# A written order for the queues of four engines, in place of the scheduler's, in a bidirectional hybrid encoder on one core

## The chip, the cores and the metric

One NeuronCore of a Trainium2 chip runs the whole program, in one launch. A core has five engines that run side by side, each taking its own queue of instructions strictly in order: TensorE (PE in the profile: matmuls, with the loads of its weights as PEld), VectorE (DVE), ScalarE (ACT), GpSimd (POOL) and SyncE (SP), whose queue here only issues transfers (DMA) from the chip's memory. Engines wait for one another by semaphores.

The metric is the device time of one execution in microseconds (us), smaller is better.

## What is computed

The reference is an encoder with two layers over a sequence of 512 tokens of width 1024, all in float32. Each layer is a token mixer and an MLP, and each adds its result to the scaled input and normalizes:

```python
for i in range(DEPTH):                       # DEPTH = 2
    if i % N_MIXERS == 0:
        m = _mixer_gdn(x, ...)               # layer 0: gated DeltaNet, 8 heads of 128
    else:
        m = _mixer_gla(x, ...)               # layer 1: gated linear attention, 4 heads, keys 128, values 256
    x = _layernorm(DEEPNORM_ALPHA * x + m, ln1_g[i], ln1_b[i])
    x = _layernorm(DEEPNORM_ALPHA * x + _sq_relu_mlp(x, mlp_w1[i], mlp_w2[i]), ln2_g[i], ln2_b[i])

def _sq_relu_mlp(h, w1, w2):                 # w1: 1024 x 4096, w2: 4096 x 1024
    a = jax.nn.relu(jnp.matmul(h, w1))
    return jnp.matmul(a * a, w2)
```

Both mixers project x, run a recurrence over the tokens in both directions (in chunks of 64 in the reference), add the two, normalize each head (RMS), multiply with a SiLU gate, and project back.

## The kernel before, in words

**Precision.** Every large matmul is done as three (`mm3`, lines 130 to 136): both operands are split into a rounded high part and a remainder, and high·high (L133), high·low (L135, or its mirror) and low·high (L136) are summed in PSUM. So each weight block comes into a buffer `wst` by a transfer that SP issues (`dma`, L46), is cast by ScalarE to `wh` (L104) and has its remainder `wl` made by VectorE (L105). `split` has a second form for blocks with a home of their own (`wb`, L98 and L99). These two steps, some hundreds of times, are the largest groups of both engines.

**Stages.** In the order of the trace: loading and transposing x with the first small projections (to 38 us); the gated DeltaNet of layer 0 with its output projection (to 430); the MLP of layer 0 (to 735); gated linear attention, GLA (to 1005); the MLP of layer 1 (to 1329); the last normalization and its stores (to 1337.6). The MLPs, and the values of GLA, use seven products of half-size blocks in place of eight, for which sums of weight blocks are made by VectorE (L485 and others) or by transfers that GpSimd issues and that add into their target (`ch`, `wst`: L1058, L1068; `w2r`: L600).

**The places that the prediction speaks of.** In the head, `ws` (L148) is a stack of high and low parts of the small weights for the projection `bap` (L154), and `xtl` (L208) the low part of the transposed x. In GDN, SP loads the blocks of the output projection, and `z`, the input again, for the residual (`load_z`, called in `output` of `gdn`); the place of z is freed by an instruction of the head that used it (`p`, L1951). In GLA, `GlaHead.levels` scales q and k for a tree of block sizes (qh L1223, kh L1226, with the running products E L1242 and F L1245), multiplies them (`scp`, L1212) and copies the result into `sc` under a mask (L1250 to L1256). `GlaHead.states` makes the states (stp L1292, copied to `st` by ScalarE at L1295, later ones by VectorE at L1298) and the outputs (op L1308); ScalarE copies each to `o` (L1310) and squares it back into its bank of PSUM (L1311), and only then can PE write to that bank, which it shares with `scp`. `GlaHead.norm` scales `o` on VectorE (L1322) by `rs` and the gate in `vs`, and PE transposes it (`otp`, L1326). `rs` comes out of a chain of small steps on VectorE and ScalarE (`rsqrt`, L243 to L260). `GlaValues.products` runs the seven products (`pjv`) with weights out of `ch`. At the end of each MLP, `layernorm` (L286 to L289) makes `xt`, which PE transposes (`tp`, L195).

**What sets the order.** The program is traced in the order in which its Python runs, with hand-made interleaving: a planner with due times in `gdn`, the tables FILL and STEPS in `gla`, generators in `mlp`. A scheduler then decides each engine's order from priorities and readiness by its own estimates. At some places the kernel takes that freedom away: `in_order(engine)` chains all instructions of one engine that were traced in its body. It stands around stretches of PE at six places, once around GpSimd's constants, once around GpSimd's work in the MLP, and once around a stretch of ScalarE there. `after` adds single waits that pace transfers. The chain that `in_order` adds is one of order alone: it has no semaphore and costs no instruction.

Of the kernel before, what the change touches and what calls it, by code (L numbers as in the profile page):

```python
# [28 lines left out]
class Ctx:  # L29
# [23 lines left out]
    def after(self, ins, before):  # L53

        self.tc.add_manual_dep(
            ins.ins, before.ins.name, mybir.DependencyInfo(mybir.DependencyClass.Sync, mybir.DependencyReason.DATA),
            reason="paced")
        return ins

    @contextlib.contextmanager  # L60
    def in_order(self, engine):
# [267 lines left out]
    def out_last(self, w, ks, lhs, z, tags, par, homes=None, xtags=("tp",), late=0, room=None):  # L329

        nc = self.nc
        homes = iter(homes or [None] * len(ks))
        ws = [[self.wrows(w, k * P, hf * 512, next(homes)) for k in ks[::2]] for hf in range(2)]
        banks = {}
        self.cols = room and (par, room)

        def part(t, hf, js):
            sl = slice(t * P, (t + 1) * P)
            if (t, hf) not in banks:
                banks[t, hf] = self.bank([P, 512], F32, name="ob", tag=tags[(2 * t + hf) % len(tags)])  # L340
                if not room:
                    nc.tensor.matmul(banks[t, hf], self.ident, z[t][hf], start=True, stop=False)
            for i in js:
                ah, al = lhs(ks[i], sl)
                wh, wl = ws[hf][i // 2]
                self.mm3(banks[t, hf], ah, al, wh[:, i % 2, :], wl[:, i % 2, :], room is not None and i == 0, i == len(ks) - 1)

        n, m = len(ks), len(ks) // 2
        with self.in_order(mybir.EngineType.PE) if late else contextlib.nullcontext():
            if late:  # L350
                for t in range(2):
                    for hf in range(2):
                        part(t, hf, range(m))
            for t in range(NT):
                for hf in range(2):
                    part(t, hf, range(m if late and t < 2 else 0, n))
                    if hf == 0 and 0 < late <= t:
                        self.xpose(t - late, self.xt[t - late], xtags)
                    if room:
                        nc.vector.tensor_tensor(self.xh(t)[hf], z[t][hf], banks[t, hf], ALU.add)  # L360
                if room:
                    self.whiten(self.xh(t))
                else:
                    self.layernorm([banks[t, hf] for hf in range(2)], self.xh(t), par, last=late and t == NT - 1)
                if not late:
                    self.xpose(t, self.xt[t], xtags)
        return [t for t in range(NT - late, NT)]


def mlp(c, w1, w2, g, b, left, before=None, out=None):  # L370
# [13 lines left out]
    with c.banks(pj=2, X=2, Y=2, Z=2), tc.tile_pool(name="mlp", bufs=2) as pool:  # L384
# [372 lines left out]
        for j, t in enumerate(left):  # L757
            for q, run in enumerate(c.xposes(t, "Y", "Z")):
                between[(2, 4 * q) if j == len(left) - 1 else (0, 4 + 3 * q)] = run
        with c.in_order(mybir.EngineType.PE), c.in_order(mybir.EngineType.Pool):  # L760
            hs = {0: h}
            tail = last(G - 1, hs)
            units = seconds(hs, tail)
            halves = c.proj_halves(specs, between)
            for f, ps in enumerate(halves):
                done = act(ps, h[0][:, f, :])
                load_part(0, 0, f // 2, f % 2, done if f > 1 else None)
                if f == 0 and before:
                    lnp.extend(c.load_ln(*before, ln_tile(), acts[0]))
                    c.cols = None  # L770
            combo = combos()
            def run(n):
                for _ in range(n):
                    next(combo, None)
            op = next(combo)
            work = pairs(op, hs)
            run(3)
            w = c.wcols(w1, GF // 2 * P)
            for f in range(4, GF):
                nw = c.wcols(w1, (f + 1) * P) if f + 1 < GF else None  # L780
                run(1 if f == 6 else 2)
                done = feature(f, h, w)
                w = nw
                if f in (4, 5):
                    load_part(0, 1, 1, f % 2, done)
                if f == 5:
                    load(0, 1, 0, acts[-1])
                if f == 6:
                    next(units)
                    next(work)  # L790
            not_done.clear()
            for _ in combo:
                pass
            with c.in_order(mybir.EngineType.Activation):
                for _ in work:
                    next(units)
                next(units, None)
            par.extend(c.load_ln(g, b, ln_tile(), acts[-1]))
            for _ in tail:
                pass  # L800


def load_x(c, x, tags, zero):
    c.new_xt()
    c.new_x()
    for t in range(NT):
        c.dma(c.xt[t], x[t * P:(t + 1) * P, :])
    idle = c.bank([P, S], F32, name="idle", tag="pj")

    def warm(n=1):  # L810
        for _ in range(n):
            c.nc.tensor.matmul(idle, zero[:, 0, :], zero[:, 0:NT, :], start=True, stop=True)

    with c.in_order(mybir.EngineType.PE):
        warm(7)
        c.marks = [c.xpose(t, c.xt[t], tags, warm=warm if t < NT - 1 else None) for t in range(NT)]
    return c.marks[-1]
# [52 lines left out]
def gla(c, gc, w_in, gate_w2, w_out, cols):  # L870
# [5 lines left out]
    with c.banks(ac=2, tp=2, X=2, Y=2), tc.tile_pool(name="gla", bufs=2) as pool, \  # L876
# [11 lines left out]
        c.dma(gst, w_in[:, base:base + 32].rearrange("(k p) n -> p k n", p=P))  # L888
        specs = [(c.stack(gst, 3), "gps", "ac")]
        specs += [(c.wcols(w_in, c0), nm, "XY"[nm == "pjk"]) for c0, nm in ((0, "pjq"), (H * P, "pjk"))]  # L890
        with c.in_order(mybir.EngineType.PE):
            gps, *qk0 = c.proj_halves(specs, dict(zip(((2, 0), (2, 4)), c.xposes(NT - 1, "tp", "tp"))))
        low = slice(64, 96)
        gl3 = pool.tile([P, S], F32R, name="gl3", tag="gl3", bufs=1)
# [19 lines left out]
        lhs = lambda k, sl: tuple(t[:, k % 4, sl] for t in o_pair(k // 4))  # L914
        early = list(range(KT // 2))
        vr = GlaValues(c, pool, w_in, heads)
        with c.in_order(mybir.EngineType.PE):
            list(heads[0].qk(qk0))
            heads[0].gates(0)
            heads[0].gates(1)  # L920
# [59 lines left out]
class GlaValues:  # L980


    ORDER = (1,2,5,6,7,4,3)
# [352 lines left out]
class GdnConst:  # L1336


    def __init__(self, c, pool, pz, w_in, a_log, dt_bias, conv_w, norm_g, behind):
# [11 lines left out]
        V.memset(self.eps[:, 1:2], math.log(0.5 * P * RMS_EPS))  # L1351
        self.ng = pool.tile([P, 1], F32, name="ng", bufs=1)
        self.cw = pool.tile([P, 5, 24], F32, name="cw", bufs=1)
        with c.in_order(mybir.EngineType.Pool):
            self.gates(w_in, a_log, dt_bias, conv_w, norm_g, behind)
            self.masks()

# [63 lines left out]
    def gates(self, w_in, a_log, dt_bias, conv_w, norm_g, behind):  # L1421

        c, pool = self.c, self.pool
# [27 lines left out]
            nc.tensor.transpose(ps[:, :120], cw, c.ident[:120, :120])  # L1451
            V.tensor_copy(self.cw, ps[:, :120].rearrange("p (k t) -> p k t", k=5))

        with c.in_order(mybir.EngineType.PE):
            ps, self.k0 = c.proj_halves([(ws, "bap", "ch"), (k0, "pjk", "ac")], {(1, 6): taps})
        yr = pool.tile([2 * M, S], F32, name="yr", tag="E", bufs=2)
        nc.scalar.copy(yr, ps[:2 * M, :])
# [501 lines left out]
        "b_gate_b", "b_norm_g", "b_w_out", "ln1_g", "ln1_b", "mlp_w1", "mlp_w2", "ln2_g", "ln2_b"]  # L1959


def body(tc, nc, a, out):
    with contextlib.ExitStack() as es:
        def pool(name, bufs, **kw):
# [2 lines left out]
        c = Ctx(tc, nc, (pool("const", 1), pool("big", 1), pool("wst", 4), pool("whl", 3), pool("small", 3)))  # L1967
        x = a["x"][0]
        with tc.tile_pool(name="gcst", bufs=1) as gp:
# [5 lines left out]
            left = gla(c, gc, a["b_w_in"][0], a["b_gate_w2"][0], a["b_w_out"][0], cols)  # L1975
        mlp(c, a["mlp_w1"][1], a["mlp_w2"][1], a["ln2_g"][1], a["ln2_b"][1], left,
            (a["ln1_g"][1], a["ln1_b"][1]), out=out[0])


# [16 lines left out]
```

## Time and profile before

| | |
|---|---|
| three runs | 1342.2, 1340.04, 1339.14 us; median 1340.04 |
| the profiled execution | 1339.26 us |
| its span in the trace | 1337.6 us (1.66 us lie around it) |
| granted TensorE clock | 0.998 |
| moved by DMA | 148.86 MB, mean 111 GB/s |

The profile is one execution, recorded instruction by instruction. A row of the timeline gives the start in us, the duration in us, the engine, the line and operation, the tile written and the tiles read (buffer numbers left out), their shapes, and the number of equal instructions that the row stands for; in brackets the idle time of the engine ahead of it and the instruction that ended it. An engine can show over 90% busy and still be fed late: the view of waits lists, for one engine, whom it stood idle for, and how long. A window row gives, for a stretch, each engine's busy us and count, the granted clock, the DMA engines' share and GB/s.

### The profile page before, as it was taken

Reading aid. Unit: us, or ns where it says so; the run is one execution under the profiler, and the core shown is the slowest. Engines: PE = TensorE matmul, PEld = TensorE weight load, DVE = VectorE, ACT = ScalarE, POOL = GpSimd, SP = SyncE. Lnnn points to the kernel's source line nnn. Section 1 sums busy time; section 2 is a strip of 40 time slices with the busy share of each in tenths; the row PEclk is TensorE's granted clock in tenths of the full one; section 3 lists DMA queues with packets and bytes.
Section 4 is the critical chain, followed back from the end, with each engine's and each line's share of the span. In section 5 each row is a group of like instructions: output and inputs, shape, how many; then the busy total and the mean of one; then the engine's idle time right before and its main releaser. Section 6 shows DMA issues by size and latency. Waiting matters only on the chain.

```text
span 1337.6 us, 22200 instructions
## 1 busy us (share of the span) xinstructions
PE 1312.5 (98%) x8726; PEld 1127.9 (84%) x8726; DVE 1127.6 (84%) x1738; ACT 777.7 (58%) x1477; POOL 118.8 (9%) x180
## 2 busy tenths in 40 slices
PE   8999999999999999999999999999999999999997
PEld 7778887888888899999998878877879899999986
DVE  6798898998768897988977889888877998889875
ACT  4766667666534656656563358647357556566640
POOL 6600000000001000101001011110000001001000
PEclk9999999999999999999999999999999999999999
DMA  7321111211133765556521666464125665556411
GB/s 196 79 64 49 49 49 48 64 46 47 52 111 110 196 135 152 130 160 160 124 83 63 183 140 158 101 152 126 44 68 156 176 173 145 139 156 129 126 63 48
DMA packets 155289, 148.86 MB, mean 111 GB/s; under 512 B 7425, under 2 KB 124193, under 8 KB 155184
## 3 DMA queue, kind: packets, MB, share of 16 engines
q1 hardware_dynamic: 144416, 115.62, 29.2%
q0 software_dynamic: 10624, 31.55, 12.6%
q8 instruction: 68, 1.11, 0.3%
q14 instruction: 37, 0.30, 0.1%
q10 hardware_dynamic: 144, 0.26, 0.1%
HBM read 118.06 MB, written 4.19 MB: 91 GB/s over the span
## 4 chain that ended last, share of the span: by engine, by line
PE 82%; DVE 7%; ACT 5%; DMA 3%; issue 2%; SPq 0%; POOL 0%; DVEq 0%; ACTq 0%; POOLq 0%
PE pq L136 6%; PE pq L133 6%; PE pq L135 6%; PE pX L135 3%; PE pX L136 3%; PE pX L133 3%; PE pjv L133 2%; PE pjv L135 2%; PE pjv L136 2%; PE pl L136 2%; PE pl L133 2%; PE pl L135 2%; PE op L1926 2%; PE lv L1789 2%; PE pY L135 2%; PE pY L136 2%
## 5 line engine op out<-in xcount | busy, mean ns | idle before, releaser
L104 ACT CAST wh<-wst 128x1024 fp32r<-128x1024 f32 (+1 forms) x175 | 173.2, 994 | 134.9 <-DVE wst L485 47.5
L105 DVE TENSOR_TENSOR wl<-wst,wh 128x1024 fp32r<-128x1024 f32 (+1 forms) x175 | 201.4, 1153 | 24.7 <-ACT wh L104 23.7
L105 DVE TENSOR_TENSOR w2l<-w2r,w2h 128x1024 fp32r<-128x1024 f32 x84 | 102.6, 1221 | 25.5 <-ACT w2h L104 25.2
L136 PE MATMUL pq<-xth,wl 128*128 128x256 f32 x384 | 108.5, 283 | 0.0
L133 PE MATMUL pq<-xth,wh 128*128 128x256 f32 x384 | 108.5, 283 | 0.0
L135 PE MATMUL pq<-xtl,wh 128*128 128x256 f32 x384 | 108.5, 283 | 0.0
L104 ACT CAST w2h<-w2r 128x1024 fp32r<-128x1024 f32 x84 | 88.1, 1049 | 5.1 <-PE pZ L136 2.6
L136 PE MATMUL pq<-t,wl 128*128 128x256 f32 x288 | 81.2, 282 | 0.4 <-DVE wl L105 0.4
L133 PE MATMUL pq<-t,wh 128*128 128x256 f32 x288 | 81.0, 281 | 0.3 <-DVE h L532 0.3
L135 PE MATMUL pq<-t,wh 128*128 128x256 f32 x288 | 81.1, 281 | 0.0
L135 PEld LDWEIGHTS pq<-xtl,wh 128*128 128x128 f32 x384 | 73.4, 191 | 3.0
L133 PEld LDWEIGHTS pq<-xth,wh 128*128 128x128 f32 x384 | 73.3, 191 | 2.9
L135 PE MATMUL pX<-w2l,ah 128*128 128x512 f32 x192 | 75.5, 393 | 0.0
L136 PE MATMUL pX<-w2h,al 128*128 128x512 f32 x192 | 75.4, 393 | 0.0
L133 PE MATMUL pX<-w2h,ah 128*128 128x512 f32 x192 | 75.1, 391 | 0.0
L136 PEld LDWEIGHTS pq<-xth,wl 128*128 128x128 f32 x384 | 73.3, 191 | 0.0
L600 POOL DMA_DIRECT2D w2r<-w2r x36 | 31.0, 877 | 404.3 <-DVE w2l L105 191.3
L485 DVE TENSOR_TENSOR wst<-wst 128x512 f32<-128x512 f32 x96 | 64.9, 684 | 0.2
L105 DVE TENSOR_TENSOR al<-h,ah 128x1024 fp32r<-128x1024 f32 x42 | 51.2, 1220 | 9.2 <-ACT ah L104 9.2
L133 PEld LDWEIGHTS pq<-t,wh 128*128 128x128 f32 x288 | 54.4, 189 | 1.6 <-DVE h L532 0.7
L135 PEld LDWEIGHTS pq<-t,wh 128*128 128x128 f32 x288 | 54.3, 188 | 1.0
L136 PEld LDWEIGHTS pq<-t,wl 128*128 128x128 f32 x288 | 54.3, 188 | 0.6 <-DVE wl L105 0.6
(557 smaller groups left out, 4049.9 us busy)
## 6 DMA issues: line engine op xcount, KB each, us to landing
wst<-in_mlp_w SPq DMA_DIRECT2D x64, 512.0 KB, 4.8
w2r<-in_mlp_w SPq DMA_DIRECT2D x64, 512.0 KB, 3.8
w2r<-w2r POOLq DMA_DIRECT2D x36, 512.0 KB, 5.6
wst<-in_a_w_in SPq DMA_DIRECT2D x32, 512.0 KB, 4.1
wst<-in_b_w_in SPq DMA_DIRECT2D x24, 256.0 KB, 3.3
wst<-in_a_w_out SPq DMA_DIRECT2D x8, 512.0 KB, 3.7
wst<-in_b_w_in SPq DMA_DIRECT2D x8, 512.0 KB, 5.5
ch<-wst POOLq DMA_DIRECT2D x8, 512.0 KB, 5.8
```

Of the source, the lines that this page charges most:

```text
L104: nc.scalar.copy(hi, src)
L105: self.low = nc.vector.tensor_tensor(lo, src, hi.bitcast(F32), ALU.subtract)
L133: mm(ps, ah, bh, start=start, stop=False, **kw)
L135: mm(ps, ah, bl, start=False, stop=False, **kw)
L136: mm(ps, al, bh, start=False, stop=stop, **kw)
L485: V.tensor_tensor(a, a, b, ALU.add)
L600: nc.gpsimd.dma_start(a, b, accum_op=ALU.add)
L1789: T.matmul(ps[:, u, :, :], lhs[:, u, :], cols(rhs, u, s, i), start=True, stop=True)
L1926: T.matmul(op[:, n, :], l, r, start=i == 0, stop=i == len(mm) - 1)
```

## The change

All uses of `in_order` are replaced by an empty context, and the freedom is taken away altogether: at the end of `body`, a new method chains all instructions of each engine in an order that is written down as a table of indices into the traced instructions of that engine. Nothing is computed in another way; the same instructions stand in both programs. The tables were found by a search that used the durations of a trace. The order of PE in the table is the one that it had.

```diff
+    def written_order(self, orders):
+
+        traced = list(self.nc.cur_bb.bb.instructions)
+        for name, text in orders.items():
+            own = [i for i in traced if i.engine == getattr(mybir.EngineType, name)]
+            ends = [[int(k) for k in run.split("-")] for run in text.split()]
+            seq = [own[k] for run in ends for k in range(run[0], run[-1] + 1)]
+            for prev, i in zip(seq, seq[1:]):
+                self.tc.add_manual_dep(
+                    i, prev.name, mybir.DependencyInfo(mybir.DependencyClass.NoSync, mybir.DependencyReason.DATA),
+                    reason="in_order")
...
-        with self.in_order(mybir.EngineType.PE) if late else contextlib.nullcontext():
+        with contextlib.nullcontext():
...
-        with c.in_order(mybir.EngineType.PE), c.in_order(mybir.EngineType.Pool):
+        with contextlib.nullcontext():
...
-            with c.in_order(mybir.EngineType.Activation):
+            with contextlib.nullcontext():
...
+ORDER = {
+    "PE": """
+        0-129 134-196 130-133 197-209 226-237 246-248 210-213 257-259 268-270 287-292 309-314 323-325 342-347 356-358
...
+    "Pool": """
+        0 2-13 15-17 19-50 52 54 56-57 63 67-68 64-66 70-72 69 73-80 58 81-96 59-62 97-131 133 132 134 137 140 135-136
...
         mlp(c, a["mlp_w1"][1], a["mlp_w2"][1], a["ln2_g"][1], a["ln2_b"][1], left,
             (a["ln1_g"][1], a["ln1_b"][1]), out=out[0])
+        c.written_order(ORDER)
```

The table has five parts: PE, DVE, Activation (ScalarE), Pool (GpSimd) and SP. From line 59 of the kernel on, the lines of the changed kernel are 12 higher (L104 becomes L116, L1322 becomes L1334).

What the tables do to the queues is read from the two programs. Three places follow; a row is a line, an operation, the tile written and the tiles read, and a shape.

ScalarE near the end of GLA, in the last head, before (in the trace at 928 to 937 us). `o` and `op` are an output of the recurrence and its bank of PSUM, `F<-wst` is the cast of a weight block of the output projection into a place where F stood:

```order
L98 CAST wb<-wst 128x1024
L104 CAST wh<-wst 128x1024
L1187 COPY k<-pjk 128x512
L1219 ACTIVATE ge<-k 128x512
L1310 COPY o<-op 128x256
L1311 ACTIVATE op,ss<-o 128x256
L104 CAST F<-wst 128x1024
L1310 COPY o<-op 128x256
L1311 ACTIVATE op,ss<-o 128x256
L1250 COPY sc<-scp 128x512
```

And in the changed kernel, the same place and, after the dots, the one where that cast now stands:

```order
L1322 COPY o<-op 128x256
L1199 COPY k<-pjk 128x512
L1231 ACTIVATE ge<-k 128x512
L110 CAST wb<-wst 128x1024
L1322 COPY o<-op 128x256
L1323 ACTIVATE op,ss<-o 128x256
L1262 COPY sc<-scp 128x512
...
L1340 ACTIVATE oth<-otp,gcol 128x512
L110 CAST wb<-wst 128x1024
L116 CAST F<-wst 128x1024
```

The cast into F, which stood between two pairs of copy and square, now comes behind the outputs' copies, the steps of `rsqrt` and the first `oth`.

VectorE in the same head, before (946 to 950 us). `rst` and `rs` are steps of `rsqrt`, the four `o` are scaled by `rs`, `xt` takes in a piece of the output projection, `qh` and `kh` are operands of the next level:

```order
L1253 COPY_PREDICATED sc<-mu_1043,scp 128x512
L259 TENSOR_TENSOR rst<-rst,rsv 128x4
L1223 TENSOR_TENSOR qh<-q,F 128x512
L325 SCALAR_TENSOR_TENSOR xt_10647<-xt_10647,oa 128x512
L260 SCALAR_TENSOR_TENSOR rs<-rst,rsy 128x4
L1226 TENSOR_TENSOR kh<-k,E 128x512
L1322 SCALAR_TENSOR_TENSOR o<-o,rs,vs 128x256 x4
L1242 TENSOR_TENSOR E<-E,F 128x2x16x16
```

And in the changed kernel:

```order
L271 TENSOR_TENSOR rst<-rst,rsv 128x4
L1265 COPY_PREDICATED sc<-mu_1036,scp 128x512
L272 SCALAR_TENSOR_TENSOR rs<-rst,rsy 128x4
L1257 TENSOR_TENSOR F<-F 128x32x2x8
L1238 TENSOR_TENSOR kh<-k,E 128x512
L1334 SCALAR_TENSOR_TENSOR o<-o,rs,vs 128x256 x4
L1235 TENSOR_TENSOR qh<-q,F 128x512
L1254 TENSOR_TENSOR E<-E,F 128x2x16x16
```

The `qh` of the next level and the piece into `xt` stood ahead of `rs` and of the four `o`; now `qh` is behind them, and `xt` is further back.

SP's queue in GDN, before, and then in the changed kernel: `wst` are the blocks of GDN's output projection (`in_a_w_out`) and of the MLP's first matrix, `z` is the input for the residual:

```order
L46 DMA wst<-in_a_w_in 128x8x128 x32
L46 DMA wst<-in_a_w_out 128x2x512 x7
L46 DMA z<-in_x 128x512 x4
L46 DMA wst<-in_a_w_out 128x2x512
L46 DMA wst<-in_mlp_w 128x8x128 x2
L46 DMA z<-in_x 128x512 x4
```

```order
L46 DMA wst<-in_a_w_in 128x8x128 x32
L46 DMA wst<-in_a_w_out 128x2x512 x3
L46 DMA z<-in_x 128x512
L46 DMA wst<-in_a_w_out 128x2x512
L46 DMA z<-in_x 128x512
L46 DMA wst<-in_a_w_out 128x2x512
L46 DMA z<-in_x 128x512 x2
L46 DMA wst<-in_a_w_out 128x2x512 x3
L46 DMA z<-in_x 128x512 x4
L46 DMA wst<-in_mlp_w 128x8x128 x6
```

The first four loads of z stood behind seven loads of weights, and the first of them now stands behind three.

More of the change, by code (lines that the diff above doesn't have):

```diff
@@ L812, in warm @@
             c.nc.tensor.matmul(idle, zero[:, 0, :], zero[:, 0:NT, :], start=True, stop=True)
-    with c.in_order(mybir.EngineType.PE):
+    with contextlib.nullcontext():
         warm(7)
@@ L890, in gla @@
         specs += [(c.wcols(w_in, c0), nm, "XY"[nm == "pjk"]) for c0, nm in ((0, "pjq"), (H * P, "pjk"))]
-        with c.in_order(mybir.EngineType.PE):
+        with contextlib.nullcontext():
             gps, *qk0 = c.proj_halves(specs, dict(zip(((2, 0), (2, 4)), c.xposes(NT - 1, "tp", "tp"))))
@@ L916, in gla @@
         vr = GlaValues(c, pool, w_in, heads)
-        with c.in_order(mybir.EngineType.PE):
+        with contextlib.nullcontext():
             list(heads[0].qk(qk0))
@@ L1353, in __init__ @@
         self.cw = pool.tile([P, 5, 24], F32, name="cw", bufs=1)
-        with c.in_order(mybir.EngineType.Pool):
+        with contextlib.nullcontext():
             self.gates(w_in, a_log, dt_bias, conv_w, norm_g, behind)
@@ L1452, in taps @@
             V.tensor_copy(self.cw, ps[:, :120].rearrange("p (k t) -> p k t", k=5))
-        with c.in_order(mybir.EngineType.PE):
+        with contextlib.nullcontext():
             ps, self.k0 = c.proj_halves([(ws, "bap", "ch"), (k0, "pjk", "ac")], {(1, 6): taps})
```

172 lines of the change are left out of this document (added).

## The prediction, made before the changed kernel was run

> **What bounds the kernel now.** I read the page first, its busy times and its chain, to learn which engine sets the end.
>
> ```profile
> span 1337.6 us, 22200 instructions
> PE 1312.5 (98%) x8726; PEld 1127.9 (84%) x8726; DVE 1127.6 (84%) x1738; ACT 777.7 (58%) x1477; POOL 118.8 (9%) x180
> PE 82%; DVE 7%; ACT 5%; DMA 3%; issue 2%; SPq 0%; POOL 0%; DVEq 0%; ACTq 0%; POOLq 0%
> ```
>
> TensorE (PE) is busy for 1312.5 of 1337.6 us, and 82% of the chain that ended last is its own. Since the change keeps TensorE's order and its instructions, it can only shorten the 25.1 us in which PE is not busy, or lengthen them. A page of the Trainium skill warns about this reading: "Perfetto Trace Analysis", section "Identifying the Most-Contended Engine", calls matmul busy time a bad measure of how far a kernel is from its roofline, because matmuls are pipelined, and asks for the busy share of the weight loads. By that share, 84%, some 209.7 us would be free (an estimate from the page's rule and the rows above). I don't use it, for the reason that the next rows show: the spacing of matmuls is set on TensorE itself.
>
> So the question is for whom PE waits. The view of the waits of PE has 21 rows with 16.1 us in all: the large ones, and of the nine small ones that I treat as one term (0.4, 0.4, 0.4, 0.3, 0.3, 0.3, 0.3, 0.2, 0.2, sum 2.8) the first and the last. The columns are us in total, times, longest.
>
> ```profile
> PE bap L154 <- DVE ws L148: 2.0, 1, 2.0
> PE gcp L1492 <- DVE gy L1487: 1.6, 1, 1.6
> PE otp L1326 <- DVE o L1322: 1.5, 2, 1.3
> PE idle L812 <- DVE pz L1509: 1.5, 1, 1.5
> PE scp L1212 <- ACT op L1311: 1.4, 1, 1.4
> PE pjv L135 <- DVE wl L105: 1.2, 2, 0.8
> PE tp L195 <- DVE xt L289: 1.1, 1, 1.1
> PE stp L1292 <- ACT st L1295: 1.1, 1, 1.1
> PE pj L136 <- DVE al L105: 0.7, 1, 0.7
> PE tp L195 <- DMA xt<-in_x: 0.6, 1, 0.6
> PE pjv L133 <- ACT wh L104: 0.4, 1, 0.4
> PE m L1904 <- ACT vn L1898: 0.4, 1, 0.4
> ...
> PE ktp L1652 <- ACT junk L1657: 0.2, 1, 0.2
> PE tp L195 <- DVE bmv L283: 0.2, 1, 0.2
> ```
>
> Hardly any of them is a DMA: PE waits for a VectorE (DVE) or ScalarE (ACT) instruction that came late. There are many short waits and no long one, so any gain must be a sum of tenths.
>
> Each wait costs a little more than the idle time says. Two matmuls that follow each other without a wait:
>
> ```profile
> 16.45 0.28 PE L135 MATMUL pjk<-xtl,wh 128*128 128x256 f32 x1
> 16.57 0.28 PE L136 MATMUL pjk<-xth,wl 128*128 128x256 f32 x1
> ```
>
> The row says 0.28 long, but the next starts 0.12 later. Where the next has to wait, that overlap of 0.16 is lost too, and no row of the waits shows it.
>
> **The change part by part.** The same instructions stand in the program on every engine; PE's order is the same word for word; the tables move 799 of ACT's 1368 instructions, 1186 of DVE's 1740, 88 of SP's 252 and 10 of GpSimd's (POOL) 185. Nothing is added that costs by itself, so every term is "a feeder of PE is reached earlier or later in its own engine's queue". Durations are those of the one profiled execution.
>
> T1, the wait of scp for op, 1.4. ACT before it:
>
> ```profile
> 934.54 1.04 ACT L104 CAST F<-wst 128x1024 fp32r<-128x1024 f32 x1 [2.07 <-DMA wst<-in_b_w_out]
> 936.45 1.16 PE L1212 MATMUL scp<-q,ge 128*128 128x128 f32 x8 [1.40 <-ACT op L1311]
> ```
>
> ACT stood idle for 2.07 us in front of a cast whose transfer had not landed, then cast for 1.04, and the read of op that PE waits for stood behind it. In the new order the cast stands eleven rows behind that read. The whole 1.4 goes; nothing waits for that weight block so soon.
>
> T2, the wait of otp for o. DVE before it:
>
> ```profile
> 946.25 0.68 DVE L1223 TENSOR_TENSOR qh<-q,F 128x512 f32<-128x512 f32 x1
> 946.85 0.68 DVE L325 SCALAR_TENSOR_TENSOR xt<-xt,oa 128x512 f32<-128x512 f32 x1
> 948.13 1.67 DVE L1322 SCALAR_TENSOR_TENSOR o<-o,rs,vs 128x256 f32<-128x256 f32 x4
> 949.45 1.16 PE L1326 MATMUL otp<-ident,o 128*128 128x128 f32 x8 [1.33 <-DVE o L1322]
> ```
>
> Both 0.68 rows, 0.6 apart in their starts, are now behind the four o. They sat ahead of the scale rs that o needs as well. That is 1.2, and the wait of 1.33 all but ends: I take 1.3 of 1.5 and leave the view's second wait, 0.2.
>
> T3, stp for st, and T4, tp for xt:
>
> ```profile
> 872.02 1.04 ACT L104 CAST wh<-ch 128x1024 fp32r<-128x1024 f32 x1 [2.57 <-DMA ch<-wst]
> 873.29 0.64 ACT L1295 COPY st<-stp 128x256 f32<-128x256 f32 x2
> 873.70 1.13 PE L1292 MATMUL stp<-vs,kdt 128*128 128x256 f32 x4 [1.05 <-ACT st L1295]
> ...
> 751.15 1.22 DVE L105 TENSOR_TENSOR wl<-wst,wh 128x1024 fp32r<-128x1024 f32 x1
> 755.77 0.66 PE L195 MATMUL tp<-ident,xt 128*128 128x128 f32 x4 [1.12 <-DVE xt L289]
> ```
>
> In both, a split of a weight block that PE needs later stood ahead of the instruction that PE was waiting for, and in the new order it stands behind. The 1.04 and the 1.22 are as long as the waits, so each goes: 1.1 and 1.1.
>
> T5, pjv for wh and for wl: 0.4 + 1.2 = 1.6.
>
> ```profile
> 799.67 1.04 ACT L104 CAST wh<-ch 128x1024 fp32r<-128x1024 f32 x1 [8.55 <-DMA ch<-wst]
> 802.02 0.50 PE L135 MATMUL pjv<-wl,cb 128*128 128x512 f32 x1 [0.76 <-DVE wl L105]
> ```
>
> ACT waits for an accumulating transfer that GpSimd issues when an earlier wl has been made and its buffer is free. DVE reaches those subtractions earlier in the new order, by one or two 128x512 operations (0.6 each). I take 1.1 of 1.6; the rest stays if GpSimd's own queue decides.
>
> T6, the nine small ones: in the new order the instructions that stood ahead of the late feeder are behind it in nearly all of them. I take 1.9 of 2.8, about two thirds.
>
> T7, bap for ws, 2.0: the feeder is moved ahead of a single 128x512 subtraction, at 0.6 apart as above, and the chain to it has links on other engines. I take 0.4.
>
> What stays: gcp 1.6, idle 1.5, al 0.7, the transfer of x 0.6, ktp 0.2 and the second otp 0.2, in all 4.8. Their feeders wait for one another or for a transfer, and nothing that could be moved stands ahead of them.
>
> The overlap: the terms rest on 17 waits (1 + 1 + 1 + 1 + 3 + 9 + 1); by what I take of each term about 13 go, at 0.16 each: 2.1.
>
> New waits: most feeders of PE that the tables push back are pushed by less than the time that lay idle between them and their matmul, so that cover hides them; I found seven at the edge, up to 0.6 each. I charge 0.9.
>
> Loads, priced at nothing: SP's queue now holds the loads of z among those of the output weights, and z waits for an early use of its place.
>
> ```profile
> 336.34 1.22 SPq L46 DMA_DIRECT2D z<-in_x  x2
> 357.57 1.05 ACT L104 CAST wh<-wst 128x1024 fp32r<-128x1024 f32 x1 [0.88 <-PE oa L136]
> ```
>
> The z loads went at 336.34, and the weight loads now behind them can't go sooner. The first of these blocks is cast at 357.57, 21 us later; even at the 8.0 that the slowest transfer quoted below took to land, that is hidden. If the cover were gone, that cast and PE behind it would be late by what is missing of one transfer, and the seven blocks after it in turn.
>
> The sum: 1.4 + 1.3 + 1.1 + 1.1 + 1.1 + 1.9 + 0.4 + 2.1 − 0.9 = 9.5. The profiled execution took 1339.26, so it becomes 1329.8. It lies 0.78 below the median of the runs shown, 1340.04, from which the same sum gives 1330.5. I forecast 1330.0.
>
> Ends of the unknown terms: if all of T1 to T7 goes (1.4 + 1.3 + 1.1 + 1.1 + 1.6 + 2.8 + 2.0 = 11.3) with an overlap of 17 × 0.16 = 2.7, no new wait comes, and a quarter of the 4.8 goes too, the gain is 15.2, which gives 1324.1 from the profiled execution and 1324.8 from the median: I write 1324.5. The other end, where terms fail, is rival A and beyond.
>
> One rule speaks against the tables themselves, which fix an order on the durations of an old one.
>
> ```profile
> L1245 DVE TENSOR_TENSOR F<-F x28: 677/690/1166, 781.5 to 962.0; 128x512 f32<-128x512 f32 x28
> ```
>
> One of these 28 equal products took 1166 ns where the median is 690, so a duration is not the operation's alone. The Trainium skill, "SBUF — State Buffer", section "Who interferes with whom", says that a VectorE instruction with two inputs in SBUF contends with a GpSimd instruction that reads SBUF, and that the one which issues second is held up. No GpSimd instruction runs at that 781.5, so the trace does not bear it out there. By that rule a reader on GpSimd with new neighbours would cost up to 1166 − 690 = 476 ns, an estimate; the sum would be 9.0 with one such. The tables move only ten GpSimd instructions, so I leave the sum.
>
> **The rivals.**
>
> A, the gain is partial because VectorE is full where the waits are. Two windows of 25 us (columns: PE, PEld, DVE, ACT, POOL busy):
>
> ```profile
> 800.00:825.00 25.00, 23.35 (x115) 18.79 (x115) 24.26 (x32) 20.51 (x34) 4.90 (x4) 1.00 0.77 164
> 1050.00:1075.00 25.00, 24.35 (x152) 21.48 (x151) 24.99 (x30) 16.42 (x23) 2.07 (x3) 1.00 0.48 105
> ```
>
> DVE has 24.26 and 24.99 of 25 us of work there. An order can't make it less: what is done earlier pushes something else back. Then T5, half of T6 and a third of the overlap stay: 9.5 − 1.1 − 1.0 − 0.7 = 6.7, and another 0.5 of new waits gives 6.2: 1333. Against it: T1 to T4, the larger terms, lie where ACT or DVE had idle time within a few us. Chance 0.18.
>
> B, no change. Each removed wait hands over to the next: the chain through DVE and ACT (7% and 5% of the span) is one of data, and a later link is late by as much. The gain is then under 2.7 us, 0.2% of 1340, which is about what a measurement of this kernel can tell from no change: so 1339, with half of that bound. For it: the waits that I keep are just of this kind. Against it: in T1 to T4 the row ahead of the late feeder has no part in its data. Chance 0.13.
>
> C, slower. An order that is written down has to take a transfer where it stands, however late it lands. The accumulating transfers for pjv are the place:
>
> ```profile
> L1068 POOL DMA_DIRECT2D ch<-wst x8: 847/877/1202, 771.2 to 870.9; - x8
>   ACT wh L104: 15.0, 4
> DMA to landing us min/median/max: 4.5/5.3/8.0
> ```
>
> ACT already waited 15.0 us for them, in four waits. One at the slow end lands 8.0 − 5.3 = 2.7 later than the median, and all that stands behind the cast on ACT, copies that PE needs among them, is late with it. To be slower by over 2.7 the kernel must lose 9.5 + 2.7 = 12.2: five of the eight at the slow end with nothing to cover them. It decides from the fifth on: 5 × 2.7 − 9.5 = 4.0 is lost, 1344. Against it: in the trace eight of the landings cost PE 1.6 in all. Chance 0.07.
>
> **How the numbers follow.** The forecast has 0.62, A 0.18, B 0.13, C 0.07. Forecast and A are both faster by over 0.2%: 0.80. Same is B, 0.13; slower is C, 0.07. The range goes from the low end, 1324.5, to 1338.0, which takes in A and the half of B in which a little is gained.
>
> **What would show it.** In the waits of PE after the change: scp for op, otp for o (the 1.3), stp for st and tp for xt are gone; gcp 1.6 and idle 1.5 are still there with the same length; the sum falls from 16.1 to 5 to 8. PE's busy time stays within 3 us of 1312.5, a little lower when the overlap counts, for the instructions are the same. The cast of F begins after the last read of op. The forecast is wrong if new rows of over 1 us stand in that view, with wl or wh as the feeder (A), if the sum stays near 16 with other names (B), or if DMA appears as the releaser of ACT's casts with PE behind (C).

## The result

| | before | new order |
|---|---|---|
| median of six runs | 1339.93 us (1339.14 to 1342.2) | 1328.76 us (1328.0 to 1329.88) |
| profiled execution, its span | 1339.26, 1337.6 us | 1328.17, 1326.1 us |
| sum of PE's waits in the profile | 16.1 us in 21 rows | 9.7 us in 11 rows |

The ratio is 0.9915, with a 95% interval of 0.9902 to 0.9928: 0.85% faster, some 11 us. The forecast was 1330.0, in a range of 1324.5 to 1338.0.

The page of the changed kernel, with the lines that answer to those shown of before:

```profile
span 1326.1 us, 22172 instructions
PE 1308.0 (99%) x8726; PEld 1129.1 (85%) x8726; DVE 1130.0 (85%) x1738; ACT 775.3 (58%) x1477; POOL 118.4 (9%) x180
PE 91%; ACT 4%; DVE 4%; DMA 1%; issue 1%; SPq 0%; DVEq 0%; ACTq 0%
```

The work of every engine is the same to within a few us; PE's busy time is 4.5 us less. What changed is the chain: PE's own share of it rises from 82% to 91%, VectorE's falls from 7% to 4%. The waits of PE, whole:

```profile
PE lv L1801 <- DVE pz L1807: 1.7, 3, 0.9
PE gcp L1504 <- DVE gy L1499: 1.6, 1, 1.6
PE bap L166 <- DVE ws L160: 1.6, 1, 1.6
PE idle L824 <- DVE pz L1521: 1.5, 1, 1.5
PE lv L1801 <- DVE Dd L1811: 1.2, 1, 1.2
PE tp L207 <- DMA xt<-in_x: 0.8, 1, 0.8
PE pj L147 <- DVE xtl L220: 0.4, 1, 0.4
PE stp L1304 <- ACT kdt L1294: 0.3, 1, 0.3
PE otp L1338 <- DVE o L1334: 0.2, 1, 0.2
PE tp L207 <- DVE rstd L272: 0.2, 1, 0.2
PE scp L1224 <- ACT op L1323: 0.2, 1, 0.2
```

Of the large rows of before, scp for op, otp for o, pjv for wl, tp for xt and stp for st are gone or down to 0.2. Two large rows are new: lv for pz and lv for Dd, 2.9 us together, both in the solve of GDN, where `lv` are PE's products and Dd, Xd and pz the operands that VectorE makes from them for the next step.

A kernel with the same matmuls in the same order allows a finer reading. Number the 8726 matmuls, take each one's start in both traces, and subtract: before minus new says how far ahead the new kernel is at that matmul. Where nothing differs the number stays flat; each place that gained or lost shows as a step. The steps hold the overlap of 0.16 as well, which the view of waits leaves out. The larger ones, with the time in before and the sum so far:

```
 before  step   so far   matmul, and whom it waited for
  12.65  +0.40  +0.30    bap for ws                        (T7)
  80.74  -0.83  -0.66    lv for pz           new
 120.18  -0.34  -1.33    lv for pz           new
 165.42  -1.03  -2.11    lv for pz           new
 206.44  -1.32  -3.31    lv for Dd           new
 273.32  +0.60  -1.73    m for vn                          (T6)
 429.74  +0.83  -0.17    pj for al
 755.77  +1.28  +1.19    tp for xt                         (T4)
 800.76  +0.68  +2.08    pjv for wh                        (T5)
 802.02  +0.94  +3.02    pjv for wl                        (T5)
 805.50  +0.62  +3.74    pjv for wl                        (T5)
 865.69  +0.59  +4.19    kdp for ge                        (T6)
 873.70  +1.22  +5.32    stp for st                        (T3)
 936.45  +1.56  +8.11    scp for op                        (T1)
 949.45  +1.50  +9.70    otp for o                         (T2)
1056.11  +0.27 +11.40    pq for wl                         (T6)
1329.18   0.00 +11.44    the last matmul
```

Steps of 0.15 and more add up to +14.9 and −5.5; smaller ones bring +2.0, which I have not followed to causes. Up to the first MLP the new order is even with the old one (−0.08 at 450 to 750 us); the whole gain is made between 750 and 1060 us, in GLA and the first part of the second MLP.

The two largest gains as rows of the changed kernel, ScalarE with PE, then VectorE with PE:

```profile
926.66 0.39 ACT L1323 ACTIVATE op<-o 128x256 f32<-128x256 f32 x1
928.34 1.06 PE L1224 MATMUL scp<-q,ge 128*128 128x128 f32 x8
945.59 1.05 ACT L116 CAST F<-wst 128x1024 fp32r<-128x1024 f32 x1
...
936.14 0.16 DVE L272 SCALAR_TENSOR_TENSOR rs<-rst,rsy 128x4 f32<-128x4 f32 x1
937.78 1.67 DVE L1334 SCALAR_TENSOR_TENSOR o<-o,rs,vs 128x256 f32<-128x256 f32 x4
939.37 0.69 DVE L1235 TENSOR_TENSOR qh<-q,F 128x512 f32<-128x512 f32 x1
939.75 1.03 PE L1338 MATMUL otp<-ident,o 128*128 128x128 f32 x8
```

No idle time in brackets stands behind either PE row: PE did not wait. The cast into F runs 19 us after the square of op, and qh runs behind the four o.

And the largest loss, ScalarE, VectorE and PE in the solve:

```profile
205.69 1.28 ACT L265 ACT_TABLE_LOAD   x1
206.98 0.21 ACT L265 ACTIVATE rsy<-rsv 128x4 f32<-128x4 f32 x1
207.21 1.28 ACT L51 ACT_TABLE_LOAD   x1
208.50 0.21 ACT L266 ACTIVATE rsy<-rsy 128x4 f32<-128x4 f32 x1
...
208.74 0.16 DVE L270 TENSOR_TENSOR rst<-rsy 128x4 f32<-128x4 f32 x1 [1.84 <-ACT rsy L266]
209.01 0.68 DVE L1811 TENSOR_TENSOR Dd<-Dd,lv 128x512 f16<-128x512 f16 x1
209.75 0.39 PE L1801 MATMUL lv<-Dd,ath 128*128 128x64 f16 x8 [1.16 <-DVE Dd L1811]
```

VectorE stands idle for 1.84 us in front of a step of 0.16, the `rst` of an earlier head's normalization, which waits for ScalarE and its two loads of an activation table, 1.28 each. Dd, for which PE waits, is queued behind it. In the old order Dd, Xd and pz stood ahead of that `rst`.

On those loads the Trainium skill, "ScalarE: Activation LUTs", section "What ACT_TABLE_LOAD costs", gives about 1283 ns and another 1380 ns of drain for each switch. The trace agrees with the first (1.28) and shows nothing of the second between these rows: `rsy` starts 0.01 us after the load ends.

### The profile page after: what moved, and what is told of

It is laid out like the page before. It is cut to its first block, busy times and chain, and to the rows that moved or that the text cites. A ratio compares the mean times of both kernels' runs of the same rounds, so it can differ in the third digit from the quotient of the medians.

```text
span 1326.1 us, 22172 instructions
## 1 busy us (share of the span) xinstructions
PE 1308.0 (99%) x8726; PEld 1129.1 (85%) x8726; DVE 1130.0 (85%) x1738; ACT 775.3 (58%) x1477; POOL 118.4 (9%) x180
## 4 chain that ended last, share of the span: by engine, by line
PE 91%; ACT 4%; DVE 4%; DMA 1%; issue 1%; SPq 0%; DVEq 0%; ACTq 0%
PE pq L148 6%; PE pq L145 6%; PE pq L147 6%; PE pX L147 3%; PE pX L148 3%; PE pX L145 3%; PE pjv L145 3%; PE pjv L148 3%; PE pjv L147 3%; PE pl L148 2%; PE pl L147 2%; PE pl L145 2%; PE pj L147 2%; PE pj L148 2%; PE pj L145 2%; PE scp L1224 2%
## 5 line engine op out<-in xcount | busy, mean ns | idle before, releaser
L116 ACT CAST wh<-wst 128x1024 fp32r<-128x1024 f32 (+1 forms) x175 | 172.6, 991 | 107.8 <-DVE wst L497 39.8
L116 ACT CAST w2h<-w2r 128x1024 fp32r<-128x1024 f32 x84 | 87.8, 1048 | 9.8 <-PE pZ L148 3.2
```

What stands on the lines that cost most here:

```text
L116: nc.scalar.copy(hi, src)
```

## The experiments

The local theory was the prediction's: the gain is a sum of waits of PE for single feeders, each of which stood in its queue behind something that could come later. Its rivals: W, that writing the order down makes the queues lighter; D, that the gain comes from transfers that go earlier; H, that the stages hand amounts on to one another; and B of the prediction, that each removed wait hands over to the next late link. All kernels have the table of PE in common. Each is compared with before on the same chip.

**1. The old order, written down.** All five tables hold what the scheduler had made of before.

```diff
 ORDER = {
-    the new order of all engines
+    the old order of all engines
 }
```

> All five tables hold the old order, so only the way of fixing it is new. Local theory (the gain is a sum of PE's waits for single late feeders): no change, 1339.9 within 0.2%, and the 21 waits of before with 16.1 us again. Rival W (writing the order down makes the queues themselves lighter, with fewer semaphore waits): a part of the 11.2 is here already, 1330 to 1337.

Measured: 1339.57, ratio 1.0002 (0.9993 to 1.0011). W falls: within 0.1%, the way of fixing an order costs and brings nothing. Between this kernel and before, the difference of the starts stays within 0.12 us from 75 to 750 us, so the method reads differences of tenths. But the waits are not the same 21 again: there are 19, with 14.0 us. With the order unchanged, three places still moved from one execution to the other: the transfer of x (+0.49), gcp for gy (+0.98) and pjv for wh (+0.44). A step at one of these three can't be put down to the order.

**2. and 3. Loads alone, and all but the loads.**

```diff
 ORDER = {                        # 2            # 3
     "DVE", "Activation":           old            new
     "Pool", "SP":                  new            old
 }
```

> SP's and GpSimd's new order, VectorE's, ScalarE's and PE's old one. Local theory: transfers were hidden, so at most the 0.8 of the wait of pj for al, 1339 to 1340. Rival D (the gain comes from transfers that go earlier): most of it is here, 1329 to 1333.

> The reverse: VectorE and ScalarE in the new order, SP and GpSimd in the old one. Local theory: nearly the whole gain, 1328.8 to 1330. Rival D: 1336 to 1340.

Measured: the new loads alone take 1343.88, ratio 1.0038 (1.0023 to 1.0053): slower, by 4.5. By its numbers D falls: the new loads alone bring no gain. "Transfers are hidden" falls as well. VectorE and the waits of PE in run 2, and a window row of run 2, then of before (busy us and count of PE, PEld, DVE, ACT and POOL, then the granted clock, the DMA share and GB/s):

```profile
385.59 1.29 DVE L337 SCALAR_TENSOR_TENSOR z<-z,oa 128x512 f32<-128x512 f32 x2 [3.74 <-DMA z<-in_x]
386.79 0.60 DVE L1895 SCALAR_TENSOR_TENSOR r<-m,neg,vt 128x128 f32<-128x128 f32 x2
...
PE m L1901 <- DVE r L1895: 2.5, 1, 2.5
...
388.60:391.90 3.30, 3.30 (x14) 2.99 (x13) 1.39 (x4) 0.15 (x1) 0.00 (x0) 0.50 0.13 34
388.60:391.90 3.30, 3.30 (x26) 3.00 (x25) 1.94 (x5) 0.53 (x2) 0.00 (x0) 1.00 0.01 2
```

VectorE stands 3.74 us in an add of z whose transfer has not landed; the recurrence's r is queued behind it, and PE waits for r. It is the second group of z loads, not the first that the prediction looked at. The new table of VectorE has these adds behind r. The step at that wait is 2.6; another 1.5 is lost in the 3.4 us from 388.5 on, in which TensorE's granted clock is 0.50 and 14 matmuls run where before has 26. Together that is 4.2 in this profile. Such a stretch at half the clock stands behind waits in other profiles too, and I come back to it with run 8.

All but the loads takes 1332.1, ratio 0.9949 (0.9932 to 0.9965): 7.3 less than before, most of the gain, but not the 11.2 of the new order. So the orders of VectorE and ScalarE bring most of it, and the new loads are needed for the rest. Its profile, at 1329.1 the fastest of its four, has one wait more than the new order's: ScalarE, VectorE and the waits of PE in the second MLP.

```profile
1028.72 1.05 ACT L116 CAST wh<-wst 128x1024 fp32r<-128x1024 f32 x1 [1.90 <-DMA wst<-in_mlp_w]
1029.80 1.22 DVE L117 TENSOR_TENSOR wl<-wst,wh 128x1024 fp32r<-128x1024 f32 x1 [1.73 <-ACT wh L116]
...
PE pq L145 <- DVE h L544: 1.5, 1, 1.5
```

In the old order of SP this weight block stands behind two loads of `w2r` and goes out at 1022.39; in the new order it stands ahead of the second of them and goes out at 1014.26. The cast waits, VectorE waits for the cast, and 15 us later h is late for PE by 1.6.

**4. and 5. The late half and the early half of the new order.** Every table is cut at what started before 600 us, in the middle of the first MLP.

```diff
 ORDER = {                        # 4            # 5
     started before 600 us:         old            new
     the rest:                      new            old
 }
```

> All tables have the old order up to the middle of the first MLP (what started before 600 us) and the new one from there. Matmul by matmul, the new kernel was 0.1 us behind the old one at that place and 11.5 ahead at the end. Local theory: 1339.9 - 11.6 = 1328.3, the whole gain comes from the GLA layer. Rival H (the early stages gained and lost amounts that a later stage hands back): between 1330 and 1335.

> The reverse of the late half: new order up to 600 us, old one behind it. Local theory: the head and GDN lose 3.8 to new waits of PE (lv for pz and Dd, ktp for vt) and win about as much in old ones (m, ktp, bap, al), so no change, 1339 to 1340.5, with the waits of lv in the profile. Rival H: at least 2 us of gain or loss.

Measured: the late half takes 1328.14, ratio 0.9916 (0.9901 to 0.9931), the early half 1339.36, ratio 0.9997 (0.9987 to 1.0006). H falls: the late half is the whole gain. In the early half the waits of lv are there as in the new order, lv for pz 1.7 and for Dd 1.2, and the steps that it wins (bap 0.40, m 0.60, al 0.83 and smaller ones) nearly make them up; this profile also has a stretch at half the clock, 1.5, behind its wait for gy.

**6. Four moves by hand in the old order.** The edit, as rows of VectorE and of ScalarE:

```diff
 L585 TENSOR_TENSOR xt_5636<-xt_5636,pl 128x512
-L117 TENSOR_TENSOR wl<-wst,wh 128x1024
...
 L301 SCALAR_TENSOR_TENSOR xt_5636<-xt_5636,rstd,ln_8651 128x512 x2
+L117 TENSOR_TENSOR wl<-wst,wh 128x1024
...
-L1235 TENSOR_TENSOR qh<-q,F 128x512
-L337 SCALAR_TENSOR_TENSOR xt_10647<-xt_10647,oa 128x512
 L272 SCALAR_TENSOR_TENSOR rs<-rst,rsy 128x4
 L1238 TENSOR_TENSOR kh<-k,E 128x512
 L1334 SCALAR_TENSOR_TENSOR o<-o,rs,vs 128x256 x4
+L1235 TENSOR_TENSOR qh<-q,F 128x512
+L337 SCALAR_TENSOR_TENSOR xt_10647<-xt_10647,oa 128x512
...
-L116 CAST wh<-ch 128x1024
 L1249 COPY E<-F 128x256
 L1307 COPY st_10171<-stp 128x256
 L1307 COPY st_10175<-stp 128x256
+L116 CAST wh<-ch 128x1024
...
-L116 CAST F<-wst 128x1024
 L1322 COPY o<-op 128x256
...
 L266 ACTIVATE rsy<-rsy 128x4
+L116 CAST F<-wst 128x1024
```

> The old order with five instructions moved by hand: the cast into F behind the outputs' copies (T1), qh and the piece into xt behind the four o (T2), one cast of ch behind two copies of st (T3), one wl behind xt (T4). Local theory: the four steps that the new order shows there, 1.56 + 1.50 + 1.22 + 1.28 = 5.6 less, 1333.9. Rival B (each wait hands over to the next late link): under 2.7 less, 1337 or more.

Measured: 1337.06, ratio 0.9984 (0.9974 to 0.9993): 2.5 less, and not 5.6. By its number this is rival B's case (under 2.7). Each move did what it should at its place (steps of +1.56, +1.07, +1.22 and +1.01), and three gave something back right behind: −1.06 at the next matmul of the new pjk, −1.15 at op, −0.39 at a scp that waits for qh. ScalarE, VectorE and PE behind the third move, and behind the fourth:

```profile
874.32 1.04 ACT L116 CAST wh<-ch 128x1024 fp32r<-128x1024 f32 x1 [1.03 <-DMA ch<-wst]
875.40 1.23 DVE L117 TENSOR_TENSOR wl<-ch,wh 128x1024 fp32r<-128x1024 f32 x1 [2.58 <-ACT wh L116]
877.90 1.65 DVE L1310 SCALAR_TENSOR_TENSOR st<-st,F,stp 128x256 f32<-128x256 f32 x4
878.82 0.70 PE L1320 MATMUL op<-vs,sc 128*128 128x256 f32 x2 [1.43 <-DVE st L1310]
...
756.02 1.22 DVE L117 TENSOR_TENSOR wl<-wst,wh 128x1024 fp32r<-128x1024 f32 x1
757.29 0.38 PE L148 MATMUL pjk<-xth,wl 128*128 128x256 f32 x1 [0.90 <-DVE wl L117]
```

The cast now comes behind the copies on ScalarE; but VectorE stands still for it in wl, 2.58 us, with the later st queued behind, and PE waits for those. And the wl that was put behind xt is itself needed soon after tp: before has the matmul that reads it 0.73 us after the start of tp, and here it starts 1.79 after. This profile also lost 1.33 at pjv for wh, of which more below; it is the slowest of the kernel's ten runs.

**10. The four moves, with what they made late.**

```diff
+L301 SCALAR_TENSOR_TENSOR xt_5636<-xt_5636,rstd,ln_8651 128x512
+L117 TENSOR_TENSOR wl<-wst,wh 128x1024
 L298 SCALAR_TENSOR_TENSOR xt_5636<-xt_5636,bmv,ln_8650 128x512
-L301 SCALAR_TENSOR_TENSOR xt_5636<-xt_5636,rstd,ln_8651 128x512 x2
-L117 TENSOR_TENSOR wl<-wst,wh 128x1024
+L301 SCALAR_TENSOR_TENSOR xt_5636<-xt_5636,rstd,ln_8651 128x512
...
-L117 TENSOR_TENSOR wl<-ch,wh 128x1024 x2
+L117 TENSOR_TENSOR wl<-ch,wh 128x1024
 L1235 TENSOR_TENSOR qh<-q,F 128x512
 L1238 TENSOR_TENSOR kh<-k,E 128x512
...
 L1310 SCALAR_TENSOR_TENSOR st_10197<-st_10189,F,stp 128x256
+L117 TENSOR_TENSOR wl<-ch,wh 128x1024
```

> The four moves by hand again, with what was then late moved too: the four later st on VectorE ahead of the wl that waits for the late cast (1.15 had been given back there), and only the first half of xt ahead of the wl that PE needs next (1.06 given back there). Completed theory (a wait goes for good where the instruction that is put behind has time, and what it blocks on the other engine is moved too): 1.01 + 1.22 + 1.56 + 1.07 - 0.39 - 0.2 = 4.3 less than before, 1335.2. Rival B: no better than the four alone, 1337.

Measured: 1335.99, ratio 0.9969 (0.9957 to 0.9980): 3.8 less than before. The loss at op has turned into a gain of 0.45 and the step at tp is the whole 1.28; what was given back is down to 0.39 for qh, 0.42 at another op, 0.40 at gps and 0.27 in the second MLP. So each theory held in part: the waits can be removed one by one, but a move pays only as far as the instruction put back, and whoever waits for it on another engine, has time. The intervals of runs 6 and 10 overlap a little (0.9974 to 0.9980); the steps at op and at the new pjk are what tells them apart. The new order is made of many such sets of moves, not of four instructions.

**11. The new loads with the adds of z moved.** Run 2 with one edit on VectorE:

```diff
-L337 SCALAR_TENSOR_TENSOR z<-z,oa 128x512 x2
 L1895 SCALAR_TENSOR_TENSOR r<-m_5406,neg,vt 128x128
...
-L337 SCALAR_TENSOR_TENSOR z<-z,oa 128x512
+L337 SCALAR_TENSOR_TENSOR z<-z,oa 128x512 x3
```

> New loads with the old order of the other engines, as in the second run, but with the two adds of z on VectorE behind the recurrence's r and sn, where the new table has them. If the 4.5 lost there came from VectorE standing 3.74 in an add of z while the recurrence was queued behind it, nearly all comes back: 1339 to 1340. If the loads cost by something else, 1342 to 1344.

Measured: 1339.39, ratio 0.9998 (0.9989 to 1.0007). All that the loads had cost comes back by moving two additions. The five tables are one thing: a part of them alone can be worse than what it replaces.

**7. The new order, mended in the solve.** At the three places on VectorE the rows that wait go behind Dd, Xd and pz; one of them, and ScalarE's part:

```diff
-L270 TENSOR_TENSOR rst<-rsy 128x4
-L271 TENSOR_TENSOR rst<-rst,rsv 128x4
 L1811 TENSOR_TENSOR Dd<-Dd,lv 128x2x16x16
 L1812 TENSOR_TENSOR Xd<-Xd,lv 128x2x16x16
 L1807 TENSOR_TENSOR pz_103<-lv,off_400 128x2x8x32
+L270 TENSOR_TENSOR rst<-rsy 128x4
+L271 TENSOR_TENSOR rst<-rst,rsv 128x4
...
-L116 CAST wh<-wst 128x1024
 L1612 ACTIVATE sil<-pjk,cw 128x512
+L116 CAST wh<-wst 128x1024
...
-L1953 ACTIVATE junk,oss<-op 128x128
 L1865 COPY vt<-ktp 128x512
+L1953 ACTIVATE junk,oss<-op 128x128
```

> The new order with the five places in GDN mended where a feeder of PE stands behind an instruction that itself waits: a cast behind sil, a copy of vt ahead of a square, and at three places the small steps of rsqrt behind Dd, Xd and pz. Local theory: the losses of 0.83 + 0.31 + 0.34 + 1.03 + 1.32 = 3.8 there come back, 1325.0. Rival B: the solve is a chain of data and the wait moves on to its next link, 1327.5 to 1328.8.

Measured: 1325.63 (1325.1 to 1326.51), ratio 0.9897 (0.9882 to 0.9912). The waits of lv are down from 2.9 to 0.6. VectorE and PE at the place of the largest loss:

```profile
206.20 0.69 DVE L1811 TENSOR_TENSOR Dd<-Dd,lv 128x512 f16<-128x512 f16 x1 [0.73 <-PE lv L1801]
207.45 0.69 DVE L1807 TENSOR_TENSOR pz<-lv,off 128x512 f16<-128x512 f32 x1
208.06 0.15 DVE L270 TENSOR_TENSOR rst<-rsy 128x4 f32<-128x4 f32 x1
...
PE lv L1801 <- DVE Dd L1811: 0.6, 1, 0.6
```

`rst` no longer waits: by the time VectorE reaches it, ScalarE is done. The steps against the new order are +0.83, +0.26, +0.34, +1.03 and +1.32, nearly all that was lost, less 0.72 at the next lv, where two other `rst` stand ahead of Dd, and 0.26 at a ktp.

**8. The old loads once more.** The kernel of run 3.

> VectorE and ScalarE new, SP and GpSimd old, once more, for a look at a slower execution: three of its four were at 1331.9 to 1333.0 and the profiled one was at 1329.1. If transfers that land late are the cause, the profile of a slow one shows a wait of PE behind a load in the second MLP, 2 to 4 us long; if not, it shows nothing there.

Measured: 1330.51, a single execution. The same wait as in run 3 is there, pq for h, now 1.7 (a step of 1.72), shorter than the 2 to 4 expected. Another 1.3 was lost between 40 and 42 us, right behind the wait for gy, and no row of the waits shows it. A window row of this run, and then of the new order:

```profile
39.80:43.00 3.20, 3.20 (x11) 2.62 (x11) 2.49 (x7) 0.70 (x2) 0.00 (x0) 0.50 0.47 137
39.80:43.00 3.20, 3.20 (x20) 2.77 (x20) 2.45 (x7) 1.59 (x3) 0.00 (x0) 1.00 0.50 143
```

The granted clock is 0.50 for 3.4 us, as in run 2. In the profiles here every such stretch, while PE still has work, begins within 2.5 us of the end of a wait of PE of about 1.6 us or more; but many waits of that length have none behind them, and what decides it stays open. These 1.7 and 1.3 are what this execution shows; no profile was taken of the three executions of run 3 at 1331.9 to 1333.0, so their cause stays open.

**9. and 12. Mended twice, beside the new order.** The two remaining `rst` behind the second solve's pz, and at the end of GDN `rstd` and the last `xt` ahead of one `xtl` each; 12 is the new order unchanged, in the same job.

```diff
+L272 SCALAR_TENSOR_TENSOR rstd<-rst,rsy 128x1
 L220 TENSOR_TENSOR xtl<-tp,xth 128x4x128
-L272 SCALAR_TENSOR_TENSOR rstd<-rst,rsy 128x1
...
+L301 SCALAR_TENSOR_TENSOR xt_5636<-xt_5636,rstd,lnp 128x512
 L220 TENSOR_TENSOR xtl<-tp,xth 128x4x128
-L301 SCALAR_TENSOR_TENSOR xt_5636<-xt_5636,rstd,lnp 128x512
```

> The mended new order with three more feeders put ahead: the two rst of the second solve behind its Dd, Xd and pz (a wait of lv for Dd of 0.72 was left there), and at the end of GDN rstd and the last xt ahead of a low part each (0.34 and 0.25). Local theory: 1.3 less than the mended one, about 1324.3. Rival B: the next link is as late, 1325.6. In both cases 3 us or more below the new order in the same job.

> The new order unchanged, in one job with the mended one for a direct comparison: 1328.8, 11 below before.

Measured: mended twice 1326.35 (1325.52 to 1327.08), ratio 0.9901 (0.9884 to 0.9917); the new order 1327.94 (1327.38 to 1329.48), ratio 0.9913 (0.9898 to 0.9927). The profile of run 12 repeats that of the changed kernel: from 16 us on, the starts of all matmuls keep within 0.17 us of one distance. Against the mended order nothing was won: mended twice was to be at 1324.3, and 3 us or more below the new order in the same job, and it is 1.6 below. The 0.72 in the solve came back; it was lost again at the end of GDN, in a wait that the mended order has not:

```profile
PE tp L207 <- DVE xtl L220: 1.0, 2, 0.6
```

PE writes its next transposes to the bank that `xtl` has still to read. So rival B held at those two moves. The best kernel of the study is number 7, about 14 us or 1.0% below before and 2 to 3 us below the new order. The intervals of its ratio and of the new order's still overlap; but the times themselves do not (1325.1 to 1327.08 for the two mended kernels, 1327.38 to 1329.88 for the new order), and the traces show the steps.

## Why the prediction was right, and where it was not

The sum was 9.5 and the measured gain 11.2; the sign, the place and the mechanism were right, but two parts were well off, in opposite directions. That the sum came this close is in part luck: the gains were taken at 10.4 with their overlap, and the steps forward are 14.9 and 2.0 of small ones; the new waits were taken at 0.9, and the steps back are 5.5.

- T1 to T4 were priced at 4.9 and, with the overlap of 0.16 each, 5.5. The steps are 1.56, 1.50, 1.22 and 1.28: 5.6. The overlap is confirmed: each of the four steps is 0.16 or 0.17 longer than the idle time in before's row.
- What the text said of T3 and T4 was wrong all the same: "a split of a weight block that PE needs later stood ahead, and in the new order it stands behind" is not enough. Run 6 made just these moves, and both gave back nearly all. The new order also has the four later st ahead of that wl, and only half of xt ahead of the other wl; with these two edits the moves kept most of their steps (run 10).
- T5 was taken at 1.1 of 1.6 for fear that GpSimd's queue decides. All three waits went: 0.68 + 0.94 + 0.62 = 2.2, of which the 0.68 at pjv for wh is not safely the order's (run 1 has +0.44 there with the old order). Rival A, that a full VectorE keeps these waits, had no part in it: the waits are gone with VectorE nearly as full (23.82 of 25 us in the changed kernel from 797 to 822 us, against 24.26 before; over the whole span 1130.0 against 1127.6). Being full in a window says nothing on which of its instructions are urgent.
- T6 was 1.9, some 2.9 with its overlap; eight of its nine waits went or shrank, with steps of 0.60, 0.59, 0.49, 0.45, 0.39, 0.36, 0.33 and 0.27, 3.5 in all. The ninth, pj for xtl, stayed and grew from 0.3 to 0.4. T7 is 0.40, as taken.
- Of what was to stay, gcp, the idle wait, the transfer of x and the second otp stayed; pj for al, 0.83, and ktp for junk, 0.38, went. The early half alone (run 5) has these two steps as well.
- New waits were charged at 0.9; the steps back of 0.15 and more make 5.5, 3.8 of it at five places in GDN (four lv of the solve, 3.5, and a ktp for vt, 0.31). This is the step that failed: "pushed by less than the time that lay idle" asks only how much work was put ahead of a feeder. At the four in the solve there is hardly more work ahead of the feeder: a row of 0.16, or a `sil`, stands there on VectorE that itself waits for ScalarE, for 0.93 to 1.84 us. What a queue does while one of its rows waits was left out, though it is what the prediction itself said of the cast into F.
- The loads were priced at nothing, and in the full change nothing of theirs shows. But the reason given was about the wrong group of z, and the cover is not 21 us of slack: it is that VectorE's table has the adds of z behind the recurrence (runs 2 and 11).
- Signs to look for: the sum of waits fell to 9.7, not to 5 to 8, because of the new waits; PE's busy time fell by 4.5, more than the 3 allowed, so it was not true that only the 25.1 us in which PE is not busy could shrink (these fell by 7.0); the cast of F came behind op; no wl or wh of over 1 us appeared.
- The row of the 28 products `F` was misread, without effect on the sum. The 781.5 is the start of the first of them and not of the one that took 1166 ns, which starts at 924.2. Four of the 28 are slow, the first level (blocks of one element) of each of the four heads: 1089 to 1170 ns in all fourteen profiles, where the other 24 take 665 to 715. So here the duration is the operation's own, and the row says nothing on contention with GpSimd.

Rival C was a transfer that lands late. Profiles with the old GLA order do show it, and those with the new order don't: among the seven with the old one (two of them with the moves by hand) pjv for wh is missing in runs 1 and 5, takes 0.2 to 0.4 in before and runs 2 and 10, 1.8 in run 6 and 1.9 in run 11; it is missing from all seven profiles with the new order there (the changed kernel, and runs 3, 4, 7, 8, 9 and 12). The row of run 11:

```profile
PE pjv L145 <- ACT wh L116: 1.9, 1, 1.9
```

Its step there is 1.46, and a stretch at half the clock behind it costs 1.3 more. In these profiles the risk that was held against the written order was one of the order that it replaced.

## What to carry to other kernels

Where one engine is busy nearly all the time (98% here) and its order is fixed, list its waits, and for each look at what stands ahead of the late feeder in the feeder's own queue; a sum of tenths was worth 0.85% here, and 1.0% after mending. Price a move by what the moved instruction will wait for, not only by how long it runs: a row of 0.16 us that waits on another engine holds its queue as long as that wait lasts, and a row that is put behind must still be on time for its own reader, on whatever engine that is. Tables of orders for several engines belong together: take them over whole, and then compare the starts of the bound engine's instructions one by one to find the few places that lost.

## What the runs showed that I had not expected

- The order of the loads alone can cost 4.5 us through one waiting row on VectorE, in a kernel whose DMA engines have a mean share of 0.42 (at that place of run 2, from 380 to 386 us, it is 0.98).
- A wait that looked fixed was not: gcp for gy is 1.6 in before's profile and in all with the new early order, but 0.4 to 0.6 in five runs with the old one and not there in a sixth. These six are the profiles in which the granted clock is low just before (0.69 from 12 to 17.5 us, and 1.00 in the other eight): PE takes 26.4 us from bap to the matmul ahead of gcp in them, and 24.9 to 25.2 in the others, and so has less to wait for gy; gcp itself starts no earlier (39.7 to 40.2 us, against 39.1 to 39.5). A shorter wait was no gain here.
- PE's busy time fell by 4.5 us with the same matmuls. So a busy share of 98% held more than the idle time let see: the time in which PE is not busy fell by 7.0 (the listed waits by 6.4), busy by 4.5, and the span by 11.5.
